# A decoder layer on one core: the pace of the row maxima, the place of their transposes, the loads of the first attention unit, and the engine of gelu's copy

## The chip, the cores and the metric

The kernel runs on one core of a Trainium2 chip. The metric is the device time of one execution in microseconds (us). The core's engines are TensorE (PE in the profile, with its weight loads listed apart as PEld), VectorE (DVE), ScalarE (ACT), GpSimd (POOL), and SyncE (SP), which issues the DMAs of this kernel. Each engine takes its instructions in the order of its own queue and waits on semaphores for the others.

## What is computed

One layer of a decoder on a sequence of 4096 tokens of width 1024, all in float32. Cut to what matters:

```python
h = rmsnorm(x, norm_g)
proj = einsum('bsd,de->bse', h, w_in)              # 3848 columns, split into 12 parts
y_a = gmlp(gelu(a_u), gelu(a_v)) * silu(a_z)       # spatial gating in chunks of 128
y_b = hgrn2(b_q, b_fl, b_i) * silu(b_z)            # gated recurrence, chunks of 128, 4 heads
# attention with a forget bias, 8 heads of 64, causal:
s = (q @ k.T) * 64**-0.5 + c[query] - c[key]       # c: running sum of log_sigmoid(c_fl + b_f)
y_c = (softmax(where(causal, s, -inf)) @ v) * silu(c_z)
out = rmsnorm(x + concat(y_a, y_b, y_c) @ w_out, final_norm_g)
```

## The kernel before

**Three phases.** Phase 1 is the input projection with the gMLP and the recurrence (0 to 1663.75 us of the span), phase 2 the attention (to 3093.5 us), phase 3 the output projection. PE's instructions stand in the order in which the program writes them (`manual_schedule` for PE); a scheduler orders those of the other engines and the DMA issues. The large products are made of three matmuls each, on a rounded part (`hi`) and a remainder (`lo`) of every operand.

**Phase 1** goes over four blocks of four token tiles T (256 tokens each) and, in each block, over 15 groups of 256 weight columns. `project` (L902, and L923 for groups laid out by features) makes one product of 48 matmuls in a PSUM tile `acc`, of which there are two; so the product after the next needs the tile that was written two products earlier, and waits until that has been copied out. After each product, generators are advanced by one step each (`tick`), the recurrence and the mixers' chains among them; they put small matmuls between the products and work on DVE, ACT and POOL. The groups `a_v` and `a_u` go through `gelu` (L741): a copy from PSUM by DVE (L744), a square by ACT, two DVE operations (L746, L747), exp, ln and exp on ACT (L728 to L730), and a DVE product (L751). The rsqrt chains of the gMLP (L97 to L104) run on DVE as well. ACT also makes `whi`, the rounded part of the next weights (L227), DVE the remainder `wlo` (L228).

**Attention** runs over 32 units, unit u = (p, Q): p is one of four pairs of heads, Q one of eight blocks of 512 queries. Unit (p, Q) has Q+1 groups, one for each block j of 512 keys; 144 groups in all. A group is eight score tiles of 128 keys by 512 queries (`do_tile`): two matmuls (L1380 with `qa` and `ka`; L1383 with `qc` and `kb`, which also brings the bias and the row maximum), then exp on ACT (L1387). After the third score tile of a group come the 16 matmuls of the previous group's product with v (`pv`, L1280). Sums of the exps over keys (`acc`, L1263) are made by DVE for one head and by POOL for the other. When a unit is done, `finish_unit` copies `pv` out, sums `acc` over partitions on PE (`pl`, L1223) and stores the result.

**Row maxima.** The softmax needs the maximum of each query's row ahead of its unit. `rowmax` finds it in pairs of products (L127, queries `qb` against keys `kb`) in a PSUM tile of two banks (`ps_sm`, two such tiles), which DVE reduces (L140; L135 for the masked diagonal ones). When all pairs of a unit are made, `rm_tail` joins them, waits for six more pairs, then transposes the maxima on PE (`mt`, L1181, in a tile of the same `ps_sm`), and DVE copies them (`mr`, L1183). Each call of `rm_step` makes one pair. It is called after score tiles n = 0, 1, 4 and 6 of every group, and after n = 3, 5 and 7 as long as the count of products `rm_count` is below `2 * si + LEAD` (si counts score tile pairs). In `do_tile`'s loop, when a unit's last group begins and the next unit's maxima are not there, pairs are forced one after another until they are (after n = 2, behind `pv`). The maxima of the first three units (`U0` = 3) are made in phase 1 by `prerm`.

**Loads.** SP issues the loads in the order that `need` gives: `kb` (256 KB and a small one), `ka` (two of 256 KB) with `v`, and per unit `qa` (twice 256 KB), `qc` (256 KB and two rows of maxima). Key tiles, `w_out` and, in phase 3, the attention's results share the 26 tiles of the pool `big`. All of the first unit's loads stand at the start of phase 2, since the pools they go to are opened there. The four tiles of `xp` (4 KB for each partition) belong to phase 1: raw x, and the operands of `prerm`.

## Time and profile before

| | |
|---|---|
| median of 3 runs | 3445.62 us (3445.28 to 3450.19) |
| the profiled execution | 3452.37 us, its span 3450.7 us |
| granted TensorE clock, mean | 0.979 |
| PE busy | 3316.0 us, 96% of the span |
| DVE busy | 2367.5 us, 69% |
| ACT busy | 1614.1 us, 47% |
| POOL busy | 1428.7 us, 41% |

In the views of the profile a busy time is the union of an engine's instructions; the idle time in square brackets stands before an instruction, with what ended it. PEclk is the clock that TensorE was granted, as a share of full speed.

### The profile page before, as it was taken

To read this page: it belongs to the slowest core of one execution; us is meant where nothing else is said; L and a number is where in the kernel's file an instruction comes from. 1 tells how busy PE (TensorE), PEld (TensorE's weight loads), DVE (VectorE), ACT (ScalarE), POOL (GpSimd) and SP (SyncE) were. 2 spreads that over 40 slices of the span, in tenths; PEclk is the share of its full clock that TensorE was granted. 3 is DMA by queue.
4 is the path that set the end of the run, shared out by engine and by line. 5 is a ranking of instruction groups with operands and counts; after the bars stand their busy time and mean duration, and the time that the engine had idled before them with its cause. 6 is when DMAs were issued, how large, how long until landed. Compare 5 with 4: busy or idle time off the path is not lost.

```text
span 3450.7 us, 62925 instructions
## 1 busy us (share of the span) xinstructions
PE 3316.0 (96%) x24375; PEld 2634.7 (76%) x24375; DVE 2367.5 (69%) x4551; ACT 1614.1 (47%) x2947; POOL 1428.7 (41%) x1504
## 2 busy tenths in 40 slices
PE   7999999999999999989899999999999999999998
PEld 7999999999999999889555555555555555548887
DVE  6467745586457855695488788888888888755554
ACT  6335553356434453354255455555555555552221
POOL 2134422243224431343266566666666666660000
PEclk9999999999999999999799999999999999999999
DMA  5332243214232133211641142014201311014442
GB/s 181 112 96 66 77 138 118 84 53 156 90 109 75 41 112 115 73 53 56 156 113 27 30 120 67 24 34 124 66 24 34 108 50 42 28 65 147 144 144 98
DMA packets 227596, 297.70 MB, mean 86 GB/s; under 512 B 19602, under 2 KB 172448, under 8 KB 227298
## 3 DMA queue, kind: packets, MB, share of 16 engines
q1 hardware_dynamic: 227298, 293.69, 28.1%
q8 instruction: 191, 3.13, 0.4%
q14 instruction: 107, 0.88, 0.1%
HBM read 208.96 MB, written 84.43 MB: 85 GB/s over the span
## 4 chain that ended last, share of the span: by engine, by line
PE 72%; DVE 18%; ACT 3%; DMA 2%; POOL 2%; issue 2%; SPq 0%; DVEq 0%; POOLq 0%; ACTq 0%
PE acc L902 16%; PE pv L1280 12%; PE acc L923 11%; PE o L1481 10%; PE st L1380 7%; PE sm L127 6%; PE st L1383 6%; DVE mp L140 3%; DVE acc L1263 3%; DVE wlo L228 2%; DMA x<-in_x_dram 2%; PE pl L1223 1%; DVE gt L746 1%; DVE xq L511 1%; PE plb L574 1%
## 5 line engine op out<-in xcount | busy, mean ns | idle before, releaser
L1387 ACT ACTIVATE pt<-st,bias 128x512 f32<-128x512 f32 (+3 forms) x1152 | 700.4, 651 | 499.0 <-PE st L1383 466.9
L1263 POOL TENSOR_TENSOR acc<-acc,pt 128x512 f32<-128x512 f32 (+2 forms) x516 | 639.0, 1238 | 303.1 <-PE st L1380 221.3
L140 DVE TENSOR_REDUCE mp<-sm 128x2 f32<-128x1024 f32 (+1 forms) x460 | 535.4, 1191 | 163.6 <-PE sm L127 163.1
L902 PE MATMUL acc<-hhi,whi 128*128 128x256 f32 x2048 | 580.0, 288 | 4.2 <-DVE q L735 2.6
L902 PE MATMUL acc<-hhi,wlo 128*128 128x256 f32 x2048 | 568.0, 282 | 0.0
L902 PE MATMUL acc<-hlo,whi 128*128 128x256 f32 x2048 | 567.4, 281 | 0.1
L923 PE MATMUL acc<-whi,hhi 128*128 128x256 f32 (+1 forms) x1792 | 518.0, 289 | 18.5 <-DVE gu L744 16.1
L923 PE MATMUL acc<-wlo,hhi 128*128 128x256 f32 (+1 forms) x1792 | 507.0, 283 | 0.0
L923 PE MATMUL acc<-whi,hlo 128*128 128x256 f32 (+1 forms) x1792 | 506.8, 283 | 0.0
L1280 PE MATMUL pv<-pt,v 128*64 128x512 f32 (+3 forms) x2304 | 503.7, 578 | 0.8 <-POOL pt L1392 0.6
L1380 PE MATMUL st<-qa,ka 128*128 128x512 f32 (+2 forms) x1152 | 466.9, 407 | 18.0 <-DMA ka<-d_kl 12.5
L1263 DVE TENSOR_TENSOR acc<-acc,pt 128x512 f32<-128x512 f32 (+2 forms) x516 | 414.4, 803 | 91.7 <-PE pv L1280 51.7
L1383 PE MATMUL st<-qc,kb 68*128 68x512 f32 (+2 forms) x1152 | 442.9, 385 | 1.4 <-DMA qc<-mr 0.8
L127 PE MATMUL sm<-kb,qb 66*128 66x512 f32 (+2 forms) x1152 | 359.2, 394 | 33.2 <-DVE mp L140 26.0
L902 PEld LDWEIGHTS acc<-hhi,whi 128*128 128x128 f32 x2048 | 384.5, 190 | 7.9 <-DVE q L735 3.0
L902 PEld LDWEIGHTS acc<-hhi,wlo 128*128 128x128 f32 x2048 | 384.4, 190 | 0.0
L902 PEld LDWEIGHTS acc<-hlo,whi 128*128 128x128 f32 x2048 | 383.9, 189 | 0.5 <-DVE hlo L290 0.3
L1280 PEld LDWEIGHTS pv<-pt,v 128*64 128x64 f32 x2304 | 158.0, 140 | 286.5 <-issue 265.0
L1380 PEld LDWEIGHTS st<-qa,ka 128*128 128x128 f32 x1152 | 220.7, 192 | 185.8 <-issue 126.1
L923 PEld LDWEIGHTS acc<-whi,hhi 128*128 128x128 f32 x1792 | 341.8, 191 | 22.3 <-DVE gu L744 16.6
L923 PEld LDWEIGHTS acc<-wlo,hhi 128*128 128x128 f32 x1792 | 342.1, 191 | 0.1
L923 PEld LDWEIGHTS acc<-whi,hlo 128*128 128x128 f32 x1792 | 341.5, 191 | 0.0
(265 smaller groups left out, 5131.9 us busy)
## 6 DMA issues: line engine op xcount, KB each, us to landing
wraw<-in_w_in_dram SPq DMA_DIRECT2D x120, 512.0 KB
x<-in_x_dram SPq DMA_DIRECT2D x88, 512.0 KB
qa<-d_qh SPq DMA_DIRECT2D x64, 256.0 KB
out_dram<-x SPq DMA_DIRECT2D x31, 512.0 KB
kb<-d_kh SPq DMA_DIRECT2D x38, 256.0 KB
d_kh<-chi SPq DMA_DIRECT2D x32, 256.0 KB
d_kl<-clo SPq DMA_DIRECT2D x32, 256.0 KB
d_qh<-chi SPq DMA_DIRECT2D x32, 256.0 KB
```

The costliest lines, as they stand in the source:

```text
L127: nc.tensor.matmul(ps[:, :n], qb[0:66, h, i * P : (i + 1) * P], kb[0:66, h, :n], start=True, stop=True)
L140: nc.vector.tensor_reduce(dst, ps, axis=AX.X, op=ALU.max)
L228: nc.vector.scalar_tensor_tensor(lo[:, k, :n], raw, g, hi[:, k, :n].bitcast(F32), op0=ALU.mult, op1=ALU.subtract)
L511: nc.vector.tensor_tensor(xq[rows, :, r, :].rearrange("p g (n h) -> p g n h", h=h), sl(e), sl(qf), op=ALU.mult,)
L902: nc.tensor.matmul(ps[:, a, :], ww[:, k, cs], hh[:, k, :], start=n == 0, stop=n == 3 * KC - 1)
L923: nc.tensor.matmul(o, hh[:, k, ts_], ww[:, k, :width], start=n == 0, stop=n == 3 * KC - 1)
L1263: ins = eng.tensor_tensor(a[:, q0:], src[:, q0:], pts[i][:, q0:], op=ALU.add)
L1280: mm = nc.tensor.matmul(pv[64 * h : 64 * h + 64, q0:], vt[:, i, 64 * h : 64 * h + 64], group[h][i][:, q0:], start=kb == 0, stop=kb == nkb - 1,
L1380: first = nc.tensor.matmul(st[:, qm:], ka_t[g][:, h, cs], qa_t[u % 2][:, h, qm:], start=True, stop=False)
L1383: nc.tensor.matmul(st[:, qm:], kb_t[g][0:68, h, cs], qc_t[u % 2][:, h, qm:], start=False, stop=True)
L1387: nc.scalar.activation(pt[:, q0:], st[:, q0:], AF.Exp, bias=bias_of[u][:, h, kb : kb + 1])
L1481: nc.tensor.matmul(ps, a[:, k % 4, o : o + P], b[k][:, cs], start=n == 0, stop=n == 3 * KC - 1)
```

## The change

1. **gelu's copy** from PSUM is made by ACT in place of DVE, for all 32 products of `a_v` and `a_u`.
2. **The first unit's operands.** The pool `xp` is opened for the whole program. A generator `preload` loads `qa`, `kb`, `ka` and `qc` of unit 0 into its four tiles, in phase 1, after `prerm`. These tiles go on as the first of the two `qa` and `qc` tiles and as the keys of unit 0; the keys of item 16 (first of the third head pair) go into two `xp` tiles too (`apart`). `big` has 24 tiles where it had 26. The tile `fgB` of phase 3 moves to `xp`.
3. **The pace.** The third kind of call of `rm_step` (n = 3, 5, 7) is made while `rm_count` is below `rm_due(si)`, worked out from a list of what must be done by when. In the first group, no pair is made after n = 0 and 1. `LEAD` grows from 76 to 88; it now sets only the order of the loads.
4. **The transposes.** A waiting tail is advanced right after a pair's products rather than ahead of the next pair's, and waits for five pairs, not six. So the transpose stands directly behind a pair.
5. `finish_unit` is advanced after n = 5, 6 and 7, not 4, 5 and 7, so that `pl` comes one score tile later.

```diff
-    xp = p1.enter_context(tc.tile_pool(name="xp", bufs=4))          # in phase 1
+    xp = ctx.enter_context(tc.tile_pool(name="xp", bufs=4))         # for the whole program
...
         def gelu(ps, dst):
-            nc.vector.tensor_copy(dst, ps)
+            nc.scalar.copy(dst, ps)
...
+        def preload():
+            for _ in range(4):
+                yield
+            for k, rows in (("qa", P), ("kb", P), ("ka", P), ("qc", 68)):
+                first_ops[k] = xp.tile([rows, 2, 512], F32R, tag="x", name=f"{k}0")
+            nc.gpsimd.memset(first_ops["qc"][64:68].bitcast(F32), 0.0)
+            load_q(0, 0, first_ops["qa"], first_ops["qc"])
+            load_keys(first_ops["kb"], 0, 0)
+            yield
+            load_m(first_ops["qc"], d_m[0])
+            load_k_hilo(first_ops["ka"], 0, 0)
...
+                if pre_on and not pre and len(pre_on) == 1:
+                    pre.append(preload())
+                    pre_on.append(True)
                 tick(pre)
...
-        big = p2.enter_context(tc.tile_pool(name="big", bufs=26))
+        big = p2.enter_context(tc.tile_pool(name="big", bufs=24))
...
                         rm_pair(ps, qb, kb_t[p * NJ + cj], hi_, cj == Q, tri, mp, cj)
+                        tick(tails)
                         yield
-                        for t in list(tails):
-                            try:
-                                next(t)
...
-            for _ in range(2 if u == 0 else 6):
+            for _ in range(2 if u == 0 else 5):
                 yield
             pt = ps_sm.tile([16, P], F32, tag="sm", name="mt")
...
-        NSLOT, NV, LEAD = 26, 10, 8 * NJ + 12
+        NSLOT, NV, LEAD = 24, 10, 8 * NJ + 24
...
+        due = [(first_step[u] - 4, 2 * first_step[u] + 8 * (Q + 1) + 16) for u, (p, Q) in enumerate(units) if u >= U0]
+        def rm_due(si):
+            return max([n - 2.5 * max(d - si, 0) for d, n in due if d >= si - 8], default=0)
...
-                if n in (0, 1, 4, 6):
+                if n in (0, 1, 4, 6) and (gi or n > 3 or not U0):
                     rm_step()
-                if n in (3, 5, 7) and rm_count[0] < 2 * si + LEAD:
+                if n in (3, 5, 7) and rm_count[0] < rm_due(si):
                     rm_step()
...
-                if n in (4, 5, 7):
+                if n in (5, 6, 7):
                     tick(fin)
```

**What moves on PE, the forced pairs.** PE in the last group of the seventh unit (group 27 of 144), before, from the product with v on; `sm` are pairs of the row maxima, `mt` their transpose, `st` score tiles:

```order
L1280 MATMUL pv<-pt,v 64x512 x8
L127 MATMUL sm<-kb,qb_21726 128x512 x6
L1181 MATMUL mt<-ident,m_24092 16x128
L127 MATMUL sm<-kb,qb_21726 128x512 x2
L1380 MATMUL st<-qa_21724,ka 128x256
L1383 MATMUL st<-qc_21729,kb 128x256
```

The same place after the change:

```order
L1316 MATMUL pv<-pt,v 64x512 x8
L1423 MATMUL st<-qa_19813,ka 128x256
L1426 MATMUL st<-qc_19816,kb 128x256
L1423 MATMUL st<-qa_19813,ka 128x512
L1426 MATMUL st<-qc_19816,kb 128x512
L149 MATMUL sm<-kb,qb_21738 128x384
L149 MATMUL sm<-kb,qb_21738 128x512
L1221 MATMUL mt<-ident,m_24103 16x128
L1423 MATMUL st<-qa_19813,ka 128x384
L1426 MATMUL st<-qc_19816,kb 128x384
```

The four forced pairs are gone from here (the group has four pairs where it had eight), and the transpose stands behind a pair with two score tiles (four matmuls) before the next. The pairs are spread: groups 1 to 4 have five pairs each after the change (seven, seven, seven and six before), group 0 three (six before), sixteen of the groups 5 to 26 five (four before), and the later groups four in both. Of the 29 transposes after the change, five stand in groups with five pairs.

PE before in a usual group with a transpose (group 48), from its first score tile:

```order
L1380 MATMUL st<-qa_21724,ka 128x512
L1383 MATMUL st<-qc_21729,kb 128x512
L127 MATMUL sm<-kb,qb_21728 128x512 x2
L1380 MATMUL st<-qa_21724,ka 128x512
L1383 MATMUL st<-qc_21729,kb 128x512
L1181 MATMUL mt<-ident,m_25874 16x128
L127 MATMUL sm<-kb,qb_21728 128x512 x2
```

Here the transpose takes one of the two PSUM tiles between two pairs, so that the second pair has to take the tile of the first, one score tile later. After the change no transpose stands in that place; it stands as in the piece of group 27 above.

**What moves on ACT.** ACT before, around the copies of the first block's `a_u` (`gt` from `gu` is the square behind the copy):

```order
L532 COPY kt<-pk 128x512
L745 ACTIVATE gt<-gu 128x512
L764 ACTIVATE gsq<-gv 128x512
L728 ACTIVATE gt<-gt 128x512
L729 ACTIVATE gt<-gt,ones_c 128x512
L730 ACTIVATE gt<-gt 128x512
L745 ACTIVATE gt<-gu 128x512
```

ACT after:

```order
L553 COPY kt<-pk 128x512
L765 COPY gu<-acc 128x512
L766 ACTIVATE gt<-gu 128x512
L785 ACTIVATE gsq<-gv 128x512
L749 ACTIVATE gt<-gt 128x512
L750 ACTIVATE gt<-gt,ones_c 128x512
L751 ACTIVATE gt<-gt 128x512
L765 COPY gu<-acc 128x512
L766 ACTIVATE gt<-gu 128x512
```

The first copy stands directly behind `kt`, no longer in DVE's queue behind the rsqrt chain; the second stands behind the exps of the first.

**What moves on SP.** At the start of phase 2, SP after the change issues `v` of unit 0 and then what unit 1 needs, among loads for the row maxima:

```order
L1183 DMA v<-d_v_97 128x4x128
L891 DMA d_v_104<-cv 128x2x256
L1188 DMA qb_21738<-d_qh_84 64x2x512
L1183 DMA v<-d_v_98 128x4x128
L114 DMA kb<-d_kh_68 64x2x512
L115 DMA kb<-d_cb_116 4x2x512
L114 DMA kb<-d_kh_69 64x2x512
L115 DMA kb<-d_cb_117 4x2x512
L114 DMA kb<-d_kh_66 64x2x512
L115 DMA kb<-d_cb_114 4x2x512
L132 DMA ka<-d_kh_66 64x2x512
L133 DMA ka<-d_kl_74 64x2x512
```

Behind these come `qa` (two) and `qc` of unit 1. Before the change, the same place held the loads of unit 0 first; these now stand in phase 1, between loads of weights and stores of the projection's results.

More of the change, by code (lines that the diff above doesn't have):

```diff
@@ L113, in load_keys, with load_q, load_m, load_k_hilo @@
         nc.sync.dma_start(t[64:68].bitcast(F32), d_cb[j][2 * p : 2 * p + 2].rearrange("h r t -> r h t"))
+    def load_q(p, Q, qa, qc):
+        nc.sync.dma_start(qa[0:64].bitcast(F32), prow(d_qh[Q], p))
+        nc.sync.dma_start(qa[64:128].bitcast(F32), prow(d_qh[Q], p))
+        nc.sync.dma_start(qc[0:64].bitcast(F32), prow(d_ql[Q], p))
+    def load_m(qc, mr):
+        for r in range(2):
+            nc.sync.dma_start(
+                qc[66 + r : 67 + r, :, :].rearrange("o h (i c) -> o (h i) c", c=P).bitcast(F32),
+                mr[8 * r : 8 * r + 8, :],
+            )
+    def load_k_hilo(t, p, j):
+        nc.sync.dma_start(t[0:64].bitcast(F32), prow(d_kh[j], p))
+        nc.sync.dma_start(t[64:128].bitcast(F32), prow(d_kl[j], p))
+    first_ops = {}
     def make_tri(tri):
@@ L1085, in tile_trunk @@
         drain(pre)
+        if U0 and len(pre_on) == 1:
+            pre.append(preload())
         drain(side)
+        drain(pre)
     nc.scalar.preload_act_table_set(LN_EXP_SET)
@@ L1102, in tile_trunk @@
         NQB = 3
-        qa_t = [qp.tile([P, 2, 512], F32R, name=f"qa{i}", tag=f"qa{i}") for i in range(2)]
+        qa_t = [qp.tile([P, 2, 512], F32R, name=f"qa{i}", tag=f"qa{i}") for i in range(1 if U0 else 0, 2)]
         qb_t = [qp.tile([66, 2, 512], F32R, name=f"qb{i}", tag=f"qb{i}") for i in range(NQB)]
-        qc_t = [qp.tile([68, 2, 512], F32R, name=f"qc{i}", tag=f"qc{i}") for i in range(2)]
+        qc_t = [qp.tile([68, 2, 512], F32R, name=f"qc{i}", tag=f"qc{i}") for i in range(1 if U0 else 0, 2)]
         tri = fs.tile([P, 512], F32, tag="tri", name="tri", bufs=1)
@@ L1111, in tile_trunk @@
             nc.gpsimd.memset(t[64:68].bitcast(F32), 0.0)
+        if U0:
+            qa_t, qc_t = [first_ops["qa"]] + qa_t, [first_ops["qc"]] + qc_t
         units = [(p, Q) for p in range(4) for Q in range(NJ)]
@@ L1115, in tile_trunk, with key_tile @@
         kb_t, ka_t, v_t = {}, {}, {}
-        def load_kb(i):
-            t = big.tile([P, 2, 512], F32R, tag="big", name="kb")
-            load_keys(t, *divmod(i, NJ))
-            kb_t[i] = t
+        apart = {i for i in (0, 2 * NJ) if U0}
+        def key_tile(i, name):
+            if i in apart:
+                return xp.tile([P, 2, 512], F32R, tag="x", name=name)
+            return big.tile([P, 2, 512], F32R, tag="big", name=name)
+        def load_kb(i):
+            if i == 0 and U0:
+                kb_t[i] = first_ops["kb"]
+                return
+            kb_t[i] = key_tile(i, "kb")
+            load_keys(kb_t[i], *divmod(i, NJ))
         def load_ka(i):
             p, j = divmod(i, NJ)
-            t = big.tile([P, 2, 512], F32R, tag="big", name="ka")
-            nc.sync.dma_start(t[0:64].bitcast(F32), prow(d_kh[j], p))
-            nc.sync.dma_start(t[64:128].bitcast(F32), prow(d_kl[j], p))
+            if i == 0 and U0:
+                t = first_ops["ka"]
+            else:
+                t = key_tile(i, "ka")
+                load_k_hilo(t, p, j)
             v = qp.tile([P, 4, P], F32, tag="v", name="v", bufs=10)
@@ L1134, in load_qb @@
             nc.sync.dma_start(qb_t[u % NQB][0:64].bitcast(F32), prow(d_qh[Q], p))
-        def load_qa(u):
-            p, Q = units[u]
-            nc.sync.dma_start(qa_t[u % 2][0:64].bitcast(F32), prow(d_qh[Q], p))
-            nc.sync.dma_start(qa_t[u % 2][64:128].bitcast(F32), prow(d_qh[Q], p))
-            nc.sync.dma_start(qc_t[u % 2][0:64].bitcast(F32), prow(d_ql[Q], p))
         mrow = {}
@@ L1166, in rowmax @@
                 yield
-                for t in list(tails):
-                    try:
-                        next(t)
-                    except StopIteration:
-                        tails.remove(t)
+                tick(tails)
         def rm_tail(u, mp):
@@ L1186, in unit_load @@
         def unit_load(u):
-            load_qa(u)
-            qc = qc_t[u % 2]
-            mr = d_m[u] if u < U0 else mrow.pop(u).bitcast(F32)
-            for r in range(2):
-                nc.sync.dma_start(
-                    qc[66 + r : 67 + r, :, :].rearrange("o h (i c) -> o (h i) c", c=P).bitcast(F32),
-                    mr[8 * r : 8 * r + 8, :],
-                )
+            if u == 0 and U0:
+                return
+            load_q(*units[u], qa_t[u % 2], qc_t[u % 2])
+            load_m(qc_t[u % 2], d_m[u] if u < U0 else mrow.pop(u).bitcast(F32))
         bias_of, acc_of, pv_of = {}, {}, {}
@@ L1290, in do_pv @@
             if Q == NJ - 1:
-                slots[0] += 2
+                slots[0] += 0 if p * NJ + j in apart else 2
                 vslots[0] += 1
@@ L1325, in load_next @@
             _, kind, i = need.popleft()
-            slots[0] -= 1
+            slots[0] -= i not in apart
             if kind:
@@ L1459, in y_split @@
             return out_
-        fgB = qp.tile([P, D], F32, tag="qa0", name="fgB")
+        fgB = xp.tile([P, D], F32, tag="x", name="fgB")
         nc.sync.dma_start(fgB, final_g[None, :].to_broadcast([P, D]))
```

2 lines of the change are left out of this document (removed).

## The prediction

> **What bounds the kernel now.** I read the page's first part first, then what PE waited for, then windows of the trace with PE's busy time and granted clock.
>
> ```profile
> PE 3316.0 (96%) x24375; PEld 2634.7 (76%) x24375; DVE 2367.5 (69%) x4551; ACT 1614.1 (47%) x2947; POOL 1428.7 (41%) x1504
> ```
>
> PE is busy for 3316.0 us of a span of 3450.7, so it is the bound, and 134.7 us of idle time are all that waits can give back, beside what the clock loses. The waits of PE over the whole span (total us, times, longest):
>
> ```profile
> PE sm L127 <- DVE mp L140: 26.0, 32, 2.1
> PE acc L923 <- DVE gu L744: 16.1, 3, 5.4
> PE st L1380 <- DMA ka<-d_kl: 12.5, 1, 12.5
> PE st L1380 <- ACT pt L1387: 5.5, 4, 3.4
> PE pl L1223 <- DVE acc L1263: 4.2, 4, 1.2
> PE pl L1223 <- ACT rt L1217: 2.4, 6, 0.7
> ```
>
> Each edit aims at a row: the pace and the transposes at the first, gelu's copy at the second, the early loads at the third, the later `pl` at the last two. Stalls have a second cost, in the clock. Windows of the attention (bounds, length, PE, PEld, DVE, ACT, POOL busy with counts, PEclk, DMA share, GB/s):
>
> ```profile
> 1735.00:3060.00 1325.00, 1288.88 (x5599) 738.01 (x5600) 1078.88 (x1535) 728.50 (x1223) 852.99 (x900) 0.99 0.22 60
> 1800.00:1900.00 100.00, 99.23 (x445) 59.10 (x445) 83.27 (x119) 55.99 (x94) 63.04 (x67) 1.00 0.12 32
> 1960.00:1970.00 10.00, 8.17 (x25) 6.42 (x26) 7.09 (x15) 3.06 (x6) 4.83 (x10) 0.56 0.03 8
> 2060.00:2070.00 10.00, 8.32 (x33) 4.09 (x33) 6.04 (x10) 3.59 (x6) 5.94 (x7) 0.83 0.36 103
> 2710.00:2720.00 10.00, 7.88 (x27) 4.67 (x27) 6.70 (x7) 5.71 (x9) 5.58 (x4) 0.78 0.23 77
> ```
>
> Between 1800 and 1900 us PE runs at 99%. The three short windows below hold stalls of about 2 us, and in each the clock is down to 0.56, 0.83 and 0.78. Over 1325 us the attention has 36.1 us of idle time and, at 0.99, some 13 us of missing clock (6.6 to 20, as 0.99 is rounded): 49 in all.
>
> **gelu's copy.** The third row of this piece of the timeline is the copy on which PE waits (start, duration, engine; idle time in brackets):
>
> ```profile
> 353.92 0.56 ACT L532 COPY kt<-pk 128x512 f32<-128x512 f32 x1
> 357.54 1.00 DVE L104 SCALAR_TENSOR_TENSOR gry<-grt,gry 128x8 f32<-128x8 f32 x1
> 359.66 0.68 DVE L744 COPY gu<-acc 128x512 f32<-128x512 f32 x1
> 360.38 0.63 ACT L745 ACTIVATE gt<-gu 128x512 f32<-128x512 f32 x1 [5.90 <-DVE gu L744]
> 360.40 0.58 PE L923 MATMUL acc<-whi,hhi 128*128 128x256 f32 x1 [5.32 <-DVE gu L744]
> ```
>
> The copy stands in DVE's queue behind an rsqrt chain, while ACT has been idle for 5.90 us. After the change ACT makes it behind `kt`, at about 354.5, for some 0.58 us (ACT's nearest row, `kt`, takes 0.56 from PSUM). PE needs it at 355.1, so the stall nearly goes. It comes in three of the four blocks, and the clock falls behind it each time:
>
> ```profile
> 360.40:370.40 10.00, 10.00 (x105) 9.80 (x106) 7.09 (x20) 3.75 (x6) 4.46 (x4) 0.83 0.03 8
> 756.00:766.00 10.00, 4.65 (x23) 4.46 (x22) 9.45 (x29) 2.08 (x4) 3.53 (x3) 0.69 0.32 98
> 1158.00:1168.00 10.00, 4.67 (x22) 4.68 (x23) 9.42 (x29) 2.38 (x4) 3.54 (x3) 0.73 0.30 93
> ```
>
> Missing clock: 1.7 + 3.1 + 2.7 = 7.5 us, of which I count 7, since some of it falls into the stall itself. So 16.1 + 7 = 23 us can go. What is late next: the second to fourth copies of a group now stand on ACT behind the previous tile's exps, which wait for DVE, busy for 9.45 of 10 us here. The buffer is needed one product later. The row of a copy on time shows nothing of that, so I bound it by nothing and by the present 5.4 us a block, and take 1.3 us in each of three blocks, near the lower end since a product of 48 matmuls lies between: 4. Gain 19 (7 to 23).
>
> In the last block the copies stand elsewhere:
>
> ```profile
> 1480.00:1580.00 100.00, 85.78 (x1001) 83.02 (x1000) 90.49 (x205) 53.25 (x98) 53.16 (x50) 0.93 0.14 39
> PE plb L574 <- DVE s L478: 8.4, 4, 3.6
> ```
>
> 14.2 us are idle and 7 of clock are missing, with DVE busy at 90%. Eight copies of 0.68 leave DVE: 5.4 us. The new loads stand here as well: 1.6 MB and nine issues on SP, ahead of loads of weights; the DMA engines are busy for 14% of this window, which hides them. If a load of weights came late by them, PE would wait for the split of its weights. Gain 4 (-4 to 12).
>
> **The start of the attention.** Windows from the start to unit 3 (bounded by the starts of units 0, 1, 2, 3), and SP's first and last issue for unit 0, with PE's wait:
>
> ```profile
> 1663.75:1676.27 12.52, 0.01 (x2) 0.03 (x1) 3.43 (x4) 0.00 (x0) 3.09 (x6) 0.66 0.85 203
> 1676.27:1689.00 12.73, 11.17 (x31) 8.93 (x31) 7.20 (x6) 4.18 (x8) 4.86 (x12) 0.50 1.07 215
> 1689.00:1718.70 29.70, 27.44 (x98) 14.53 (x96) 20.19 (x38) 11.42 (x20) 13.84 (x21) 0.78 0.83 179
> 1718.70:1753.00 34.30, 32.27 (x134) 18.40 (x133) 27.00 (x42) 15.52 (x26) 15.94 (x18) 0.90 0.55 127
> 1663.78 0.59 SPq L1138 DMA_DIRECT2D qa<-d_qh  x1
> 1671.76 0.57 SPq L1127 DMA_DIRECT2D ka<-d_kl  x1
> 1676.27 0.77 PE L1380 MATMUL st<-qa,ka 128*128 128x512 f32 x1 [12.52 <-DMA ka<-d_kl]
> ```
>
> The stall does not go, it moves behind unit 0. That unit runs at once, but unit 1 needs what SP issues up to its `qc`: two `v`, one store, one `qb`, three `kb`, two parts of `ka`, three of `qa` and `qc`, about 12 times 256 KB, or 3.2 MB. The DMA engines are saturated here at 203 to 215 GB/s, so these take 15 us and land near 1680. Unit 0 is done by about 1668 (eight masked tiles and three pairs, 4 us at full clock), so PE waits 12 us once more, and unit 1 starts at 1680 and not 1689. From there the rows price the rest. Work at full clock from unit 1 to unit 3: 27.44 x 0.78 + 32.27 x 0.90 = 50.4 us, less seven pairs that groups 1 to 4 no longer have. A pair is two matmuls, and matmuls of 512 columns start 0.235 us apart (the third row is a product with v, used below):
>
> ```profile
> 1950.53 0.39 PE L1380 MATMUL st<-qa,ka 128*128 128x512 f32 x1
> 1950.76 0.40 PE L1383 MATMUL st<-qc,kb 68*128 68x512 f32 x1
> ...
> 1954.74 3.65 PE L1280 MATMUL pv<-pt,v 128*64 128x512 f32 x16
> ```
>
> So 0.47 a pair, 47.1 us of work; 3 us of idle time (4.3 before), and a loss of clock of 14: the half clock held for all 12.7 us of the second window and into the third, some 22 us, and I expect it as long after the new stall (11 lost), with 3 for later dips. Unit 3 then starts near 1744, 9 us early, and nine pairs in all, 4.2 us, are made later instead. Gain 5 (-3 to 16; the upper end if the clock comes back early, as the stall has work ahead of it).
>
> The Trainium skill ("DMA: Bandwidth & Descriptors", Specifications) gives about 358 GB/s as one core's limit at the memory. By that figure the 3.2 MB would land in 9 us, near 1674, and I would estimate some 6 us more of gain. The rows above disagree: 215 GB/s with every DMA engine busy.
>
> **The steady attention.** The costliest wait has this form; the pair before, the transpose, two reductions, and the pair that waits:
>
> ```profile
> 2058.90 0.63 PE L127 MATMUL sm<-kb,qb 66*128 66x512 f32 x2
> 2059.84 0.27 PE L1181 MATMUL mt<-ident,m 128*16 128x128 f32 x1
> 2060.52 1.22 DVE L140 TENSOR_REDUCE mp<-sm 128x2 f32<-128x1024 f32 x1
> 2061.79 0.74 PE L127 MATMUL sm<-kb,qb 66*128 66x512 f32 x2 [1.68 <-DVE mp L140]
> ```
>
> The transpose has one of the two tiles of `ps_sm`, so the pair behind it must wait until the pair one score tile earlier has been reduced: 1.22 us and about 0.3 for the handover, against 0.47 of score tile and 0.27 of transpose. That makes 0.8, as the first row of the waits has it (26.0 / 32); here DVE was late besides. After the change two score tiles and the transpose lie between, 1.2 us: 0.3 to 0.35 remain, in 24 transposes 8 us. In the five that stand in groups of five pairs, the transpose itself waits for a pair 0.94 us earlier, 0.6 each: 3. Next, these groups: four pairs leave DVE 83.27% busy; a group lasts 9.3 us (24 matmuls of score tiles and pairs at 0.235, and `pv` 3.65), so DVE has 7.8 us of work, with the fifth pair 9.0 in 9.8, 92%. The price of one such group lies between nothing and one wait of 0.8; I take 0.3, since groups of four show almost none, in 20 groups 6. The forced pairs of group 27 and their low clock (the 1960 row) go. `pl` moves behind most of its waits (6.6 in the rows above). Where DVE splits the output weights, and elsewhere, I leave 4, and for clock 5. Sum after: 8 + 3 + 6 + 4 + 5 = 26 of 49. Gain 23 (5 to 42).
>
> **The end of the attention.**
>
> ```profile
> 3060.00:3093.50 33.50, 27.29 (x92) 12.73 (x90) 15.53 (x17) 15.26 (x25) 22.15 (x21) 0.80 0.20 63
> ```
>
> 6.2 us idle, most of it the row `PE st <- ACT pt` above: exps queued behind casts of phase 3 that wait for DVE. With 24 tiles of `big`, these casts come a group later. Gain 3 (-3 to 6). In phase 3 itself the fewer tiles cost nothing as long as the casts for a token tile are done within the products of the previous one; now PE never waits there:
>
> ```profile
> 3150.00:3350.00 200.00, 200.00 (x884) 165.66 (x883) 106.09 (x301) 45.01 (x90) 0.00 (x0) 1.00 0.40 142
> ```
>
> **Sum.** 19 + 4 + 5 + 23 + 3 = 54. The profiled execution took 3452.4 us, which makes 3398; it lies 6.8 above the median, so for the median 3445.6 - 54 = 3391.6. I say 3391.
>
> **Rivals.**
> 1. *DVE becomes the bound in the groups of five pairs.* At 92% its late work adds up: each of the 20 groups then loses a wait of 0.8 and half the clock of some 1.8 us behind it, 1.7 in all, 34 us and not 6. For it: 27.00 of 34.30 us and short waits on DVE already where groups had seven. Against: PE at 99% with DVE at 83%. Gain 26, 3420. Chance 0.13.
> 2. *Short stalls cost no clock.* Then the low clock of the three short windows has another cause and stays, and with it 8 of the 13 us that I let go. Gain 46, 3400. The low clock stands behind a stall in each window, which speaks against it. Chance 0.08. The Trainium skill ("TensorE: Matmul & The Clock Gate", What's actually happening) has that rule: half clock after an idle window of about 3.4 us, full clock after as much busy time. The trace disagrees twice: 0.83 behind a stall of 1.68 us, and 0.50 for 12.7 us of work behind the long one.
> 3. *gelu's change does not do what it says.* The stall only moves to the later copies, behind exps that wait for the same late DVE. Gain 54 - 19 = 35, 3411. Chance 0.06. Together with the first rival it leaves 7, no change that can be told.
> 4. *Slower: the same queue, at every copy.* ACT is in order, so a copy behind a waiting exp holds PE whenever DVE's part of gelu takes longer than a product. Three of four copies in each of two groups in each of four blocks stand so: 24. At 4 us each (the present stalls are 5.3) 96 us, against 35 of the other gains: 61 slower, 3507. It decides once the copy ends over one product after its own product's last matmul; a product is 48 matmuls, which start about 0.12 us apart, so some 6 us:
>
> ```profile
> 353.79 0.28 PE L923 MATMUL acc<-wlo,hhi 128*128 128x256 f32 x1
> 353.91 0.28 PE L923 MATMUL acc<-whi,hlo 128*128 128x256 f32 x1
> ```
> For it: DVE at 94 to 95% beside `a_u`. Against: the `kt` row and ACT's 5.90 us of idle time; at `a_v` PE does not wait now though DVE has these copies. Chance 0.07.
>
> **Numbers.** My forecast has 0.66. Its terms' bounds combined as independent ones (12, 8, 8, 18, 6 down, 4, 8, 11, 19, 3 up: roots of the sums of squares 25 and 24) give 3367 to 3416 of its own. The range reaches to the first rival and a little beyond on both sides: 3363 to 3428. About 0.2%, or 7 us, is what a measurement of this kernel can tell from no change. Faster: 0.66 + 0.11 + 0.08 + 0.03 = 0.88; same: 0.05, where the first and third rivals meet; slower: 0.07.
>
> **What would show it.** In the profile after: no row of PE `acc` waiting for `gu` over 4 us in total (else the third or fourth rival); a wait of PE for unit 1's operands of about 12 us near 1670, with the half clock behind it; in the attention's window PE's idle time down from 36 to about 21, with PEclk nearer to 1.00, and DVE busy for 90% or more in groups 5 to 26; no stall where group 27 was. I am wrong if the waits on `mp` keep their total, if the stall at the start vanishes altogether, or if PE waits in phase 3.

## The result, and the profile after

The changed kernel takes 3432.03 us (median of 5 runs, 3428.64 to 3433.44), the kernel before, measured with it, 3450.19 (3445.28 to 3454.14). The ratio is 0.9949, with a 95% interval of 0.9934 to 0.9963: faster by 0.5%, 18 us, where 54 were forecast. The profiled execution took 3431.63 us with a span of 3429.9, 20.8 us shorter than the span before. The first part of the changed kernel's page:

```profile
PE 3305.2 (96%) x24375; PEld 2639.0 (77%) x24375; DVE 2350.4 (69%) x4519; ACT 1634.0 (48%) x2979; POOL 1429.3 (42%) x1504
```

PE is busy for 10.8 us less and idle for 10.0 us less than before. Its longest waits over the whole span (total, times, longest), without those of the first 40 us:

```profile
PE plb L595 <- DVE s L499: 14.9, 8, 3.6
PE st L1423 <- DMA qa<-d_qh: 14.8, 2, 10.1
PE acc L944 <- ACT gu L765: 12.0, 6, 2.5
PE sm L149 <- DVE mp L162: 11.4, 21, 0.9
PE mt L1221 <- DVE mp L162: 9.2, 5, 3.2
...
PE pl L1259 <- DVE acc L1299: 5.9, 4, 2.0
```

Every wait that the change aimed at has left a wait behind. The pairs wait 11.4 us where they waited 26.0, but transposes, which never waited long before, wait 9.2 in five places. gelu's copy costs 12.0 where it cost 16.1, in six stalls where there were three. The wait for the first unit's operands (12.5) is now one of 14.8 for later units. The sums `pl` wait 6.6 us in all (5.9 for DVE, 0.7 for ACT), as long as before (4.2 and 2.4), so the later step of `finish_unit` won nothing. And a wait at which the change did not aim has grown: PE waits 14.9 us for a step of the recurrence on DVE (`plb`), where it waited 8.4.

Where the time went shows best by stages of the attention. Windows of the kernel before, bounded by the starts on PE of unit 0, unit 3, unit 7 and the last group (length; PE, PEld, DVE, ACT, POOL busy; PEclk; DMA share; GB/s):

```profile
1676.27:1753.04 76.77, 70.92 (x259) 41.90 (x260) 54.42 (x84) 31.15 (x54) 34.67 (x49) 0.79 0.74 162
1753.04:1968.11 215.07, 209.69 (x913) 122.93 (x912) 179.90 (x252) 115.58 (x194) 133.59 (x140) 0.98 0.19 49
1968.11:3076.00 1107.89, 1074.37 (x4649) 611.23 (x4648) 890.91 (x1262) 612.74 (x1028) 717.13 (x755) 0.99 0.22 61
```

The same stages of the changed kernel:

```profile
1655.04:1742.06 87.02, 65.53 (x241) 40.05 (x242) 49.87 (x67) 30.63 (x54) 37.41 (x53) 0.75 0.70 153
1742.06:1979.96 237.90, 226.74 (x933) 132.22 (x932) 191.23 (x277) 118.11 (x194) 131.76 (x137) 0.91 0.17 44
1979.96:3057.20 1077.24, 1055.07 (x4647) 610.39 (x4646) 888.23 (x1258) 617.44 (x1029) 722.53 (x759) 0.99 0.23 62
```

Three things are to be read here. Unit 0 starts 21.2 us earlier, but the first stage is 10.2 us longer. The stage from unit 3 to unit 7 (groups 6 to 27) is 22.8 us longer, at a clock of 0.91 where it was 0.98. The long rest is 30.6 us shorter. Together with 2.0 us behind the start of the last group, the gains add up to 53.8 us, and the two stages that became longer gave 33.0 of them back within 325 us.

The loss in groups 6 to 27 at its first place, group 8 (start, duration, engine; idle time in brackets):

```profile
1763.75 0.20 POOL L185 TENSOR_TENSOR mm<-mm,cref 128x8 f32<-128x8 f32 x1
...
1764.23 0.17 DVE L192 SCALAR_TENSOR_TENSOR m<-mm,m 128x8 fp32r<-128x8 f32 x1 [1.82 <-ACT m L191]
...
1764.31 2.35 DVE L162 TENSOR_REDUCE mp<-sm 128x2 f32<-128x1024 f32 x2
...
1766.58 4.90 DVE L1299 TENSOR_TENSOR acc<-acc,pt 128x512 f32<-128x512 f32 x4
...
1767.97 5.97 POOL L1299 TENSOR_TENSOR acc<-acc,pt 128x512 f32<-128x512 f32 x4 [4.03 <-PE st L1423]
...
1768.84 0.63 PE L149 MATMUL sm<-kb,qb 66*128 66x512 f32 x2
...
1771.40 2.34 DVE L162 TENSOR_REDUCE mp<-sm 128x2 f32<-128x1024 f32 x2
...
1772.67 0.38 PE L1221 MATMUL mt<-ident,m 128*16 128x128 f32 x1 [3.20 <-DVE mp L162]
```

And a window of the time behind the last row:

```profile
1772.67:1784.62 11.95, 11.95 (x31) 7.26 (x33) 7.17 (x9) 3.80 (x6) 2.15 (x4) 0.50 0.17 47
```

DVE waits 1.82 us for a step of the maxima that runs over POOL and ACT, so it reduces the group's first two pairs late, and makes its four sums late. They now run beside POOL's sums and take 4.90 us. The next two pairs on PE have been made meanwhile, and the transpose behind them needs the tile of the first of them, whose reduction begins only at 1771.40. PE stands still for 3.20 us, and then runs for 12 us at half clock (0.50, while busy throughout).

### The profile page after: what moved, and what is told of

The parts are those of the page before. It is cut to its first block, busy times and chain, and to the rows that moved or that the text cites. A ratio compares the mean times of both kernels' runs of the same rounds, so it can differ in the third digit from the quotient of the medians.

```text
span 3429.9 us, 62893 instructions
## 1 busy us (share of the span) xinstructions
PE 3305.2 (96%) x24375; PEld 2639.0 (77%) x24375; DVE 2350.4 (69%) x4519; ACT 1634.0 (48%) x2979; POOL 1429.3 (42%) x1504
## 4 chain that ended last, share of the span: by engine, by line
PE 76%; DVE 14%; ACT 3%; POOL 3%; DMA 2%; issue 2%; SPq 0%; DVEq 0%; POOLq 0%; ACTq 0%
PE acc L923 16%; PE acc L944 14%; PE pv L1316 12%; PE o L1524 10%; PE st L1423 7%; PE sm L149 7%; PE st L1426 6%; DVE mp L162 3%; DVE acc L1299 2%; DVE wlo L249 2%; DMA x<-in_x_dram 1%; POOL acc L1299 1%; PE pl L1259 1%; PE plb L595 1%; DVE xq L532 1%
## 5 line engine op out<-in xcount | busy, mean ns | idle before, releaser
L944 PE MATMUL acc<-whi,hhi 128*128 128x256 f32 (+1 forms) x1792 | 517.0, 288 | 12.5 <-ACT gu L765 12.0
L1423 PE MATMUL st<-qa,ka 128*128 128x512 f32 (+2 forms) x1152 | 471.8, 412 | 21.0 <-DMA qa<-d_qh 14.8
L149 PE MATMUL sm<-kb,qb 66*128 66x512 f32 (+2 forms) x1152 | 360.2, 395 | 18.6 <-DVE mp L162 11.4
```

Of the source, the lines that this page charges most:

```text
L149: nc.tensor.matmul(ps[:, :n], qb[0:66, h, i * P : (i + 1) * P], kb[0:66, h, :n], start=True, stop=True)
L944: nc.tensor.matmul(o, hh[:, k, ts_], ww[:, k, :width], start=n == 0, stop=n == 3 * KC - 1)
L1423: first = nc.tensor.matmul(st[:, qm:], ka_t[g][:, h, cs], qa_t[u % 2][:, h, qm:], start=True, stop=False)
```

## The experiments

All of them were timed beside the kernel before, whose medians lay between 3448.7 and 3450.7 us. Runs that were timed at different moments are compared by their ratios to it.

**Run e1: gelu's copy back on VectorE**

```diff
-            nc.scalar.copy(dst, ps)
+            nc.vector.tensor_copy(dst, ps)
```

> The changed kernel with gelu's copy back on VectorE, all else as changed. The changed kernel took 3432. If the copy on ScalarE brought what the two traces show (PE's idle time for gu 16.1 against 12.0 us, windows of half clock behind it 17 against 10 us), this run is 6 to 9 us slower, 3438 to 3441, with three stalls of 5.3 us back. The prediction's term would make it 19 slower, 3451. If the stall only moved to later copies and nothing was won, it is 3432.

Measured: 3439.07 us, ratio 0.997 (0.9959 to 0.9982); the three stalls of 5.4 us (16.1 in all) are back. So the copy on ACT brings 7 us, not 19. What is left of it shows in the first block of the changed kernel:

```profile
355.81 0.39 PE L944 MATMUL acc<-whi,hhi 128*128 128x256 f32 x1 [1.54 <-ACT gu L765]
...
360.32 0.92 DVE L768 TENSOR_SCALAR gt<-gt 128x512 f32<-128x512 f32 x1
...
361.28 0.63 ACT L749 ACTIVATE gt<-gt 128x512 f32<-128x512 f32 x1 [3.17 <-DVE gt L768]
...
364.92 1.26 POOL L810 TENSOR_TENSOR m<-m,gu 128x512 f32<-128x512 f32 x1
...
366.21 0.59 ACT L765 COPY gu<-acc 128x512 f32<-128x512 f32 x1 [2.88 <-POOL m L810]
...
366.85 0.39 PE L944 MATMUL acc<-whi,hhi 128*128 128x256 f32 x1 [2.46 <-ACT gu L765]
```

ACT waits 3.17 us for DVE's part of the first tile before it can make the exps that stand ahead of the second copy. They are done at 363.33, a microsecond before PE needs the copy (364.39). But the copy waits 2.88 us more, until GpSimd has multiplied the first tile into `m` (to 366.18), and PE waits with it. `gu`, `gv` and `gz` share four tiles, so the copy probably writes into the tile that this product reads; the trace shows the wait and not its reason.

**Run e2: transposes kept off close pairs**

```diff
             for _ in range(2 if u == 0 else 5):
                 yield
+            while not t_ok[0]:
+                yield
...
+                if n == 0:
+                    close = False
+                t_ok[0] = n == 6 or (n == 4 and not close)
...
                 if n in (3, 5, 7) and rm_count[0] < rm_due(si):
+                    close = True
                     rm_step()
+                t_ok[0] = True
```

> The changed kernel with one rule more: a transpose goes behind a pair only where two score tiles or the product with v lie on both sides of that pair, so in groups of five pairs it goes behind the last pair. The pace is the changed one. Theory: the loss between groups 6 and 27 lies in five transposes, each directly behind two pairs close together, where the transpose waits 2 to 3 us for a reduction that stands in VectorE's queue behind its four sums, and the clock is halved behind it. Then 9 us of waits and about 20 us of the half clock's loss go: 3403 to 3412. Rival: the groups of five pairs make VectorE the bound whatever stands where; then the waits show up at the pairs instead, and the time is 3428 or more.

Measured: 3418.38 us, ratio 0.9909 (0.9895 to 0.9922). That is 14 us faster than the changed kernel, between the two expectations. PE's waits of this run from unit 3 to unit 7:

```profile
PE sm L149 <- DVE mp L162: 5.4, 5, 2.3
PE sm L149 <- DVE mp L157: 2.4, 1, 2.4
PE mt L1224 <- DVE mp L162: 1.2, 3, 0.4
```

That stage's window:

```profile
1742.60:1969.50 226.90, 217.62 (x933) 126.79 (x932) 190.81 (x277) 117.75 (x194) 131.71 (x137) 0.96 0.17 46
```

The transposes wait 1.2 us, but pairs wait 5.4 behind the same late reductions. The stage is 11.0 us shorter than in the changed kernel and 11.8 longer than before the change. Moving the transposes takes away half of the loss. The other half belongs to the groups of five pairs themselves, as the next run and e5 bear out.

**Run e3: the old pace, with the same rule for the transposes**

```diff
-                if n in (0, 1, 4, 6) and (gi or n > 3 or not U0):
+                if n in (0, 1, 4, 6):
...
-                if n in (3, 5, 7) and rm_count[0] < rm_due(si):
+                if n in (3, 5, 7) and rm_count[0] < 2 * si + 8 * NJ + 12:
```

> The changed kernel with the old pace (seven pairs in groups 1 to 3, four in the later ones, forced pairs now and then) and the rule of the run before for the transposes; so no group of five pairs after group 5. Theory (the transposes' place was the loss): groups 6 to 27 are as quick as in the run before or a little quicker, the first four groups slower by their more numerous pairs and waits, in sum within 5 us of that run, 3405 to 3415. Rival (five pairs in a group are too many for VectorE): this run is faster than the run before by 15 us or more.

Measured: 3426.63 us, ratio 0.9936 (0.9924 to 0.9949), slower than either expectation. The total hides two opposite parts, which the stages show:

```profile
1737.30:1950.70 213.40, 208.25 (x908) 121.60 (x907) 177.59 (x247) 116.22 (x194) 134.03 (x142) 0.98 0.18 49
1950.70:3052.50 1101.80, 1073.17 (x4653) 612.05 (x4653) 899.50 (x1267) 614.42 (x1028) 718.61 (x756) 0.98 0.21 61
```

One piece of its timeline, in the last unit:

```profile
2988.28 0.77 PE L1429 MATMUL st<-qc,kb 68*128 68x512 f32 x1 [1.64 <-DMA qc<-mr]
```

Without groups of five pairs, groups 6 to 27 take 213.4 us and not 226.9: the rival was right there. From group 28 on, the run takes 1101.8 us where the changed pace takes 1077.2: with the old pace the maxima come just in time, pairs are forced in two more groups, and `qc` once arrives too late for its unit (last row). That is 6 us less than in the kernel before, but e10 below, with the old pace and the transposes in their old place, takes 1100.0. So the transposes' new place wins nothing from group 28 on by itself; the changed pace is what wins there.

**Run e4: unit 0's store issued later**

```diff
             nc.gpsimd.tensor_tensor(t, t, r, op=ALU.mult)
+            for _ in range(9 if u == 0 else 0):
+                yield
             nc.sync.dma_start(d_yc[p][Q], t)
```

> The changed kernel, but the store of unit 0's result is issued nine steps of its finish later. Theory: the wait of 10.1 us for unit 2's operands in the changed kernel comes from SP, which stood 13.8 us in front of that store, which waited for GpSimd, which waited for the load of z, with DMA engines idle for 7 us of it; without it unit 2 starts some 8 to 10 us earlier and a window of half clock (13.7 us long) shrinks: 3414 to 3424. Rival: the data come no earlier since the DMA engines are full until then: 3430 to 3434.

Measured: 3425.91 us, ratio 0.9932 (0.992 to 0.9945), 6 us faster than the changed kernel, just above the theory's range. In the changed kernel SP, POOL and PE stand like this:

```profile
1681.30 0.26 SPq L115 DMA_DIRECT2D kb<-d_cb  x1
...
1692.29 1.28 POOL L1268 TENSOR_TENSOR rt<-rt,zt 128x512 f32<-128x512 f32 x1
...
1695.08 0.34 SPq L1272 DMA_DIRECT2D d_yc<-rt  x1
...
1697.44 0.58 SPq L119 DMA_DIRECT2D qa<-d_qh  x1
...
1703.51 0.77 PE L1423 MATMUL st<-qa,ka 128*128 128x512 f32 x1 [10.10 <-DMA qa<-d_qh]
```

SP issues nothing between 1681.30 and 1695.08, and unit 2's `qa` stands behind the store. With the store moved, the same start of unit 2 is in that run:

```profile
1697.72 0.76 PE L1425 MATMUL st<-qa,ka 128*128 128x512 f32 x1 [3.77 <-DMA qa<-d_qh]
```

The wait of 10.10 us is 3.77. What is left of it falls into a stretch in which the DMA engines are full (busy share 1.04 at 214 GB/s between 1690 and 1697.7 us).

**Run e5: a pace of its own, early pairs and few groups of five**

```diff
-                if n in (0, 1, 4, 6) and (gi or n > 3 or not U0):
+                if n in (0, 1, 4, 6):
...
-                if n in (3, 5, 7) and rm_count[0] < rm_due(si):
+                if n in (3, 5, 7) and rm_count[0] < (2 * si + 8 * NJ + 18 if gi < 6 else rm_due(si)):
```

on top of e2.

> The changed kernel with the rule that keeps transposes off close pairs, and a pace of its own: seven pairs in groups 1 to 4 and six in groups 0 and 5, as early as in the kernel before, then the changed rule, which now asks for five pairs only in groups 24 to 26. Theory: pairs made beside the loads of the first units are nearly free, and a fifth pair in a later group costs about 1 us over its own 0.5; then this run joins the lead that the old pace has at group 28 (17 us) to the 33 us that the changed pace wins from there to the end: 3398 to 3408. Rival: a pair costs its 0.5 us wherever it stands, and only the transposes' place counted; then it is as the run with that rule alone, 3413 to 3419.

Measured: 3406.72 us, ratio 0.9872 (0.9859 to 0.9886), as the theory had it. Its stages:

```profile
1655.60:1740.70 85.10, 73.16 (x265) 43.68 (x266) 62.73 (x93) 31.71 (x55) 38.20 (x54) 0.78 0.76 163
1740.70:1953.00 212.30, 208.22 (x910) 120.40 (x909) 176.27 (x251) 116.60 (x193) 130.93 (x137) 0.98 0.18 47
1953.00:3028.10 1075.10, 1051.80 (x4648) 607.75 (x4647) 889.85 (x1258) 617.21 (x1029) 722.68 (x759) 1.00 0.22 62
```

The first stage holds twelve pairs more than that of the changed kernel (40 against 28) and is 1.9 us shorter: beside the loads these pairs cost nothing. The second stage, with three groups of five pairs and not fifteen, is 25.6 us shorter; twelve pairs fewer are 5.6 of them.

**Run e6: only the first copy of each block on ScalarE**

```diff
-            nc.scalar.copy(dst, ps)
+            (nc.scalar.copy if first else nc.vector.tensor_copy)(dst, ps)
...
-            gelu(ps, u)
+            gelu(ps, u, T % BT == 0)
```

> The changed kernel with gelu's copy on ScalarE for the first tile of a_u in each block alone, and on VectorE for all others. Theory: the changed kernel's stalls of 2.5 us come from the second copy, which stands on ScalarE behind the first tile's exps, and those wait for VectorE; on VectorE it is on time, as before the change. Then three stalls of 2.5 us and the half clock behind them (three windows of 3.4 us) go: 3420 to 3427. Rival: VectorE's backlog is what is late, and the second copy waits there as long: 3430 to 3435.

Measured: 3435.44 us, ratio 0.9958 (0.9946 to 0.9971). The time is the rival's (a little over its 3435). PE's waits in phase 1 of this run:

```profile
PE acc L944 <- DVE gu L765: 12.9, 3, 4.3
...
PE acc L944 <- ACT gu L765: 2.0, 3, 0.7
```

The first stall falls to 0.7 us, and the one on the second copy grows to 4.3: together 5.0 a block, against 4.0 in the changed kernel. The second copy in the first block:

```profile
364.95 1.26 POOL L810 TENSOR_TENSOR m<-m,gu 128x512 f32<-128x512 f32 x1
...
366.24 0.69 DVE L765 COPY gu<-acc 128x512 f32<-128x512 f32 x1 [2.15 <-POOL m L810]
```

DVE makes it at 366.24, as ACT did (366.21), and stands idle for 2.15 us ahead of it. So what holds it last is not a queue of the copying engine but GpSimd's product of the first tile. DVE's backlog comes in earlier, in the first tile's own chain (the 3.17 us above).

**Run e7: the early loads alone**

The changed kernel with gelu's copy, pace, `LEAD`, transposes and finish of the kernel before.

```diff
-            nc.scalar.copy(dst, ps)
+            nc.vector.tensor_copy(dst, ps)
...
-                        tick(tails)
                         yield
+                        tick(tails)
...
-                if n in (5, 6, 7):
+                if n in (4, 5, 7):
```

and the two lines of e3's diff.

> The kernel before with the early loads of the first unit alone; gelu's copy, pace, transposes and the finish as before, and PE's order with them. The kernel before takes 3449. Theory: the stall of 12.5 us is not gone but comes again in smaller waits before units 1 and 2, since the DMA engines stay full; but the early pairs fill part of it: 5 to 8 us faster, 3441 to 3444. Rival: the store of unit 0 in SP's queue and the full DMA engines give all of it back, 3447 to 3451. Were the stall simply gone, with its half clock, it would be 3425 to 3432.

Measured: 3429.11 us, ratio 0.9944 (0.9931 to 0.9958): 21 us faster than the kernel before, as much as the whole change. My theory and its rival are both refuted; the time lies where it was expected if the stall were simply gone. Its first stage:

```profile
1659.60:1738.80 79.20, 68.74 (x259) 40.35 (x260) 58.19 (x87) 31.17 (x54) 36.46 (x53) 0.83 0.78 169
```

It is 2.4 us longer than before the change, where the changed kernel gives back 10.2. With the old order PE has seven pairs a group to make while the next unit's operands arrive, and no wait for `qa` comes. The start is not all of the 21 us, though: PE's wait ahead of unit 0 falls from 12.5 to 0.8 us, and less the 2.4 that makes 9.3.

**Run e8: e5, e6 and e4 together**

> Three edits to the changed kernel together: the pace and the transposes' rule of the first run of this call, the copy of the second run, and unit 0's store issued later. If they add up: 3398 to 3408 by the first, 5 to 10 less by the second, and the store up to 5 less (the old early pace waits less for unit 2): 3386 to 3400. If the first rival holds, 3400 to 3412.

Measured: 3403.93 us, ratio 0.9865 (0.9851 to 0.9878), not told apart from e5 and in the rival's range. The copy brings nothing, as in e6, and the store nothing that shows: with this pace little of the wait is left to win (in the first stage PE waits 1.9 us for `qa` in e5, and 14.8 in the changed kernel).

**Run e9: gelu's last product on GpSimd**

```diff
-            nc.vector.tensor_tensor(dst, dst, t, op=ALU.mult)
+            nc.gpsimd.tensor_tensor(dst, dst, t, op=ALU.mult)
```

> The changed kernel with gelu's last product on GpSimd in place of VectorE (0.68 us off VectorE for each of the 32 tiles); the copy stays on ScalarE. Theory: what holds the copies back is VectorE's backlog beside a_u, which reaches ScalarE's queue through the exps; with 2.7 us less on VectorE for each of a_v and a_u in a block, the two stalls of each block (1.5 and 2.5 us) shrink by about half and with them the half clock: 3422 to 3428. Rival: the copies wait for something else in ScalarE's queue (the split of the weights): 3430 to 3435. GpSimd's slower product could also hold up the chain of a_v: over 3436.

Measured: 3454.05 us, ratio 1.001 (1.0001 to 1.0019), 21 us slower than the changed kernel, as the third expectation had it (over 3436). PE's longest waits in phase 1 of this run:

```profile
PE plb L595 <- DVE s L499: 24.7, 7, 6.4
PE acc L944 <- ACT gu L765: 14.0, 6, 3.6
```

The work that left DVE did not shorten the stalls on `gu` and lengthened another, for a step of the recurrence. That a lighter DVE would have helped is not shown, as the chain of `a_v` became longer by the same edit.

**Run e10: without pace, transposes and finish**

The changed kernel with the two lines of e3's diff, `LEAD` of 76, and the tails and the finish of e7's diff; gelu's copy stays on ACT.

> The changed kernel without its parts on the pace, the transposes and the finish: PE's order in the attention is that of the kernel before, the early loads and gelu's copy on ScalarE stay. If the parts add up, this is the run with the loads alone less the 7 us of gelu's copy: 3420 to 3425, some 10 us faster than the changed kernel, so that pace and transposes together cost 10 us. If they paid as forecast, it would be 3445 or more.

Measured: 3423.96 us, ratio 0.9922 (0.9909 to 0.9934), as expected. Loads (21 us) and copy (7) add up; pace, transposes and finish together cost 8 to 9 us. From group 28 on this run looks so:

```profile
1950.50:3050.50 1100.00, 1068.24 (x4649) 609.13 (x4649) 889.64 (x1262) 612.95 (x1028) 722.27 (x757) 0.99 0.22 61
```

It is 7.9 us shorter than before the change with the old pace and the old place, and 22.8 longer than in the changed kernel.

**Run e11: e5 with e4's store and e9's product**

> The pace of its own and the transposes' rule (the run e5), the late store of unit 0, and gelu's product on GpSimd. If gelu's stalls shrink as in the first run of this call, 5 to 10 us below the 3407 of e5: 3396 to 3403. If they do not: 3403 to 3408.

Measured: 3425.0 us, ratio 0.9926 (0.9913 to 0.9938), slower than both expectations. Against e5, the product on GpSimd costs 18 us here.

**Run e12: e5's pace, transposes as before the change**

```diff
-                        tick(tails)
                         yield
+                        tick(tails)
...
-            for _ in range(2 if u == 0 else 5):
+            for _ in range(2 if u == 0 else 6):
```

on the changed kernel with e5's two lines and without e2's rule.

> The pace of its own of run e5, pair for pair the same, but the transposes again ahead of a pair, after six pairs, as in the kernel before. With this pace they stand ahead of a group's first pair in most cases, two score tiles behind the last pair, and not between two pairs one tile apart as before the change. Theory: what costs is a distance of one score tile between the pairs around a transpose, not the side on which it stands; then this is as e5 within 6 us, 3401 to 3413. Rival: standing directly behind a pair is what wins; then the waits of the kernel before come back, some 14 us of them from group 28 on: 3418 to 3428.

Measured: 3394.96 us, ratio 0.9847 (0.9833 to 0.986), the best of all, 54 us faster than the kernel before, and faster than either expectation. Standing directly behind a pair is not what wins. Its last two stages:

```profile
1740.50:1949.40 208.90, 204.80 (x908) 119.56 (x906) 175.69 (x248) 116.37 (x193) 130.22 (x137) 1.00 0.18 48
1949.40:3018.60 1069.20, 1049.56 (x4648) 606.37 (x4648) 886.15 (x1260) 615.51 (x1029) 725.08 (x759) 1.00 0.22 63
```

PE's wait for `pl` in this run, between 1730 and 3045 us (in e5 it is 6.9 us, in six stalls):

```profile
PE pl L1259 <- DVE acc L1299: 1.7, 2, 1.1
```

With e5's pace, a transpose that stands ahead of a pair has two score tiles or the product with v between the pairs around it, as in e5; before the change there was one. So it is the distance that counts. Why `pl` waits less with the transposes ahead of the pairs is not shown.

## Why the prediction was wrong

The direction was right, and the size was off by a factor of three. The spans differ by 20.8 us, and stage by stage the sum went like this:

| stage | forecast | measured |
|---|---|---|
| phase 1 (gelu and the last block) | 23 | 9.5 (its end at 1654.2, before at 1663.75; in e1, with the copies on DVE, at 1661.0) |
| its end to unit 3 | 9 | 1.4 (12.52 less 0.84 of waiting, less 10.25 of the longer stage) |
| unit 3 to the last group, with the 4.2 us of pairs put off | 19 | 7.8 (-22.8 and +30.6) |
| from the last group to the end | 3 | 2.0 (374.7 to 372.7) |

**gelu.** The step that failed is the residual: "take 1.3 us in each of three blocks". It measured 4.0 a block, 12.0 in all: 1.5 on the first copy, ahead of which ACT still makes splits of weights and `kt`, and 2.5 on the second. For the second the text had named a cause (copies behind exps that wait for DVE), and rival 3 had it as its whole mechanism; I priced it near its lower end because a product lies between. The exps were late, but the wait that ended last was one that the working did not have, for GpSimd's product of the first tile. Run e6 shows that it is the same whichever engine copies, and in e9, with 0.68 us a tile less on DVE but a longer chain for `a_v`, it did not become shorter. Whether one more tile for `gu` would have removed it was not tried. The slower rival's mechanism (a copy held in ACT's queue) is in the trace too, at one copy a block and not at 24.

Two smaller terms of gelu fell short as well. The 7 us of clock did not all come back: the 10 us behind the second copy still have a clock of 0.83 in each of the three blocks, a loss of 1.7 us each. And of the 4 us that eight copies less on DVE were to bring in the last block nothing shows: between 1480 and 1580 us PE's idle time fell from 14.2 to 11.2, but it is 11.8 in e1 too, where DVE makes the copies. The waits for `plb` are 8.2 us in e1 and 14.9 with the copies on ACT; why is open. In all, e1 gives the copy 7 us, where 23 were forecast for phase 1.

**The start.** "PE waits 12 us once more" was right in kind: 2.9 us in unit 0, and 14.8 for the operands of units 1 and 2 (4.7 and 10.1). Unit 1 began 16.4 us behind the end of phase 1 (at 1670.6), as the working had it (1663.75 to 1680). But the working stopped at unit 1's loads and did not follow SP's queue on to the store of unit 0, which held unit 2's `qa` back (e4: 6 us). And it took it that pairs taken out of the first groups save their time there. Runs e5 and e7 show the contrary: beside the loads, twelve pairs cost nothing, so putting pairs off saved nothing and left PE idle. With the old pace the start alone is worth 9.3 us (e7), where the sum had 5 and the changed kernel has 1.4. The other gains of e7 lie elsewhere: some 6 us of its 21 fall near 2700 us, where the splits of the output weights stand otherwise with 24 tiles; what part of that is the tiles' was not tried.

**Groups of five pairs.** The step "the transpose itself waits for a pair 0.94 us earlier, 0.6 each: 3" failed most. It took it that DVE is free when the pair is made. Four of the five waits are 1.7 to 3.2 us (9.2 in all), since DVE's queue then holds three or four late sums. The low clock costs more still: 0.91 over the stage of 237.9 us is 21 us of missing clock, most of it behind these waits, and 0.98 over 215.1 was 4. Without the transposes in that place the stage is 11.0 us shorter (e2). "I take 0.3 [...] in 20 groups 6" was too small as well: e2 has fifteen such groups in this stage and e5 three, with the same rule for the transposes, and e2's stage is 14.6 us longer. Twelve pairs are 5.6 of that, so a group of five costs 0.75 besides its pair, near the upper bound of 0.8. It is not DVE's share of busy time that shows this: DVE was busy for 191.23 of 237.90 us, 80%, where the working had 92; it was late at single moments. The first rival had these groups at 34 us in place of 6, a gain of 26; with the third it left 7. The measured 18 lies between, and both happened in part.

**From group 28 on.** The gain was larger than the forecast for the whole attention: 30.6 us. Of what I named, the wait at the transposes did go. But e3, e10 and e12 show that the pace makes the difference. With the old pace the stage takes 1100.0 us with the transposes in the old place (e10) and 1101.8 in the new (e3); with a pace that runs ahead of need and the old place it takes 1069.2 (e12). So 8 of the 30.6 us come without pace and place. That the pace decides at which step of a group a transpose falls, and whether maxima arrive in time, the working did not see. It forecast that these waits would go and put it down to the transposes' new place, so here it was right by luck.

**The clock.** The second rival (short stalls cost no clock) has the trace against it: the clock was 0.50 for 12 us behind the stall of 3.20, and two more transposes that waited 1.97 and 1.93 us show it as well, in these windows of the changed kernel:

```profile
1826.00:1840.00 14.00, 12.03 (x35) 6.80 (x35) 9.73 (x11) 4.49 (x7) 5.65 (x7) 0.63 0.01 3
1890.00:1904.00 14.00, 12.07 (x35) 6.84 (x35) 9.83 (x11) 4.49 (x8) 5.96 (x7) 0.64 0.01 2
```

Each window holds one stall and about 5 us of lost clock. The Trainium skill ("TensorE: Matmul & The Clock Gate", Why this matters for your kernels) warns of idle gaps above about 3 us; here 2 us were enough, though PE had been busy without a break, at full clock, for the 10 us before the first of them (1816 to 1826).

## What to carry to other kernels

Work that can be moved in time is cheapest beside a transfer that the main engine must wait for anyway; before spreading it evenly, find out what it stands beside now. When a step needs what another engine makes, price its wait by that engine's queue at that moment (the late sums, the backlog), not by the step's own distance or by the engine's share of busy time; and when a load is made early, follow the issuing queue to the next load that is needed, past every store that waits for something. And compare stages, not totals: here a loss of 22.8 us and a gain of 30.6 lay one behind the other in one change.

## What the hardware showed besides

DVE's sums were slower beside POOL's. In the piece of group 8 above, DVE's four sums take 4.90 us while POOL makes its own. One by one, the second and third of them and POOL's first are:

```profile
1767.29 0.69 DVE L1299 TENSOR_TENSOR acc<-acc,pt 128x512 f32<-128x512 f32 x1
1768.02 1.80 DVE L1299 TENSOR_TENSOR acc<-acc,pt 128x512 f32<-128x512 f32 x1
1767.97 1.28 POOL L1299 TENSOR_TENSOR acc<-acc,pt 128x512 f32<-128x512 f32 x1 [4.03 <-PE st L1423]
```

Ahead of POOL's first sum DVE takes 0.68 and 0.69 us; the two beside POOL's take 1.80 and 1.63. The third begins 0.05 us after POOL's first and ends 0.57 after it. From unit 3 to the last group of the changed kernel (1742 to 3057 us) it is the same: 273 of DVE's sums of 512 columns lie beside no two-operand instruction of POOL that takes over 0.5 us, and these take 0.69 us on average, none over 0.77; 35 lie beside one for at least nine tenths of their time and take 1.55. So a DVE that is late and comes beside POOL's sums becomes later by another 2 us.

The Trainium skill ("SBUF — State Buffer", SBUF: two separate sides) has VectorE with two operands in SBUF and GpSimd take turns at one pair of ports, one blocking the other for a whole instruction. The rows agree with that: the sum that begins 0.05 us behind POOL's is done 0.57 us after POOL's has ended, near its own 0.69 us.
